# Hybrid decoder trunk: in the third and eleventh up panel, both chunk pairs with seven products stand one chunk later

## The chip, the cores and the metric

The kernel runs on one core of one Trainium2 chip. The metric is the device time of one execution in microseconds (us); for the kernel before it is the median of 3 runs. All arithmetic is fp32.

## What is computed

Two layers over 256 tokens of width 2048, each with attention beside a cross-attention over 256 memory tokens, and then a channel mixer. Only the channel mixer bears on the change:

```python
def conv_ffn(h, w_up, conv_w, conv_b, w_down):
    u = causal_dwconv(h @ w_up, conv_w, conv_b)      # width 3 over the tokens
    a, val = split_cols(u, [FFN_HIDDEN, FFN_HIDDEN])  # 5632 each
    return (jax.nn.silu(a) * val) @ w_down

def reference(...):
    for i in range(DEPTH):                            # DEPTH = 2
        ...                                           # attention adds to x
        h = rmsnorm(x, norm_ffn[i])
        x = x + conv_ffn(h, ffn_w_up[i], ffn_conv_w[i], ffn_conv_b[i], ffn_w_down[i])
    return rmsnorm(x, norm_final)
```

## The kernel before

**Three matmuls for one product.** Both factors are kept as a rounded part ("hi") and the rest ("lo"). A product takes hi times hi, lo times hi and hi times lo, three matmuls. The activations are kept so already (buffers A and B, 16 chunks of 128 rows). The weights are split as they arrive: SyncE's queue (SP) loads a chunk into a slot of the ring `raws` (L246, or L455 for a pair), ScalarE makes hi (L256, or L404), VectorE makes lo (L257, or L405). The rings have slots of 128 x 1024 words: in the mixer eight for raw weights (five and three guests) and six each for hi and lo.

**Up panels.** The up-projection of a layer is done in eleven panels, `up_pair(j)` for j = 0, 4, ..., 40. Each computes 512 columns of `a` and 512 of `val` (two halves `h_`) for 256 tokens (two blocks `b`), and takes the 16 chunks of the contraction one after the other. The third panel is j = 8, the eleventh and last j = 40. Panels 0 to 16 come first, then two down panels (`down_pair`), then panels 20 to 28 and so on; after panel 40 come the last down panels.

**Pairs with seven products.** An ordinary chunk k takes four products (2 blocks by 2 halves) of three matmuls, 12 in all. Two chunks k and k+1 that stand in `sums` are taken together by Winograd's form of Strassen's scheme: seven products p1 to p7 of three matmuls, 21 instead of 24. Its weight sums are built on VectorE in place in the pair's two raw slots `ra` and `rb` (L461 to L464), and there are four splits (`split_more`, L404 and L405): `w1` and `w2` of the weights as they are, `w3` and `w4` of the sums. `w3` feeds p5 and p7, `w4` feeds p6 and p4. The sums of the activations (`usum`) were made ahead. Panels with j // 4 in `MORE_IN` (1, 2, 5 to 10) take two pairs, (6,7) and (11,12), the others one, (6,7).

**Where the pairs stand.** `pair_steps` lays down the order of the chunks. Its argument `ahead` says how far ahead of its own place a pair is taken:

```python
        while at < n:
            if at + ahead in sums:
                plan.append(at + ahead)
                at += 2
            else:
                plan.append(single.pop(0))
                at += 1
```

`up_pair` passes `2 * second`: 2 in a panel with two pairs, otherwise 0.

**Banks and ends of a panel.** Eight PSUM banks are used: the products p1, p5, p7, p6 ("fast") in four of them and p2, p3, p4, x ("slow", into which the ordinary chunks also go) in the other four. `flip` exchanges the two sets from panel to panel, so that the fast products of the third and the eleventh panel lie in `ps_o`, `ps_s`, `ps_s`, `ps_t`, where the slow ones of the next panel go. After the last pair `early` adds up the fast banks (L1527 to L1534); after the last chunk `late` adds each slow bank (L1538), and VectorE turns the blocks (L1489). GpSimd's queue writes the turned blocks to DRAM (L674) and reads them back in another order (L679).

**Conv work.** What a panel has produced is convolved and gated in the next panel and beyond: 12 tap products on ScalarE for each half (L1442), two adds on VectorE (L1449), the silu (L1455) and the gating (L1462 and the split L552 and L553). `tick(share)` hands out these steps after each yield of `pair_steps`: after an ordinary chunk a share of 1.7 (panels with two pairs) or 1.45, after a pair two ticks with a share of 0. A half costs 10.2 shares. Its steps come due 7 or 8 ticks after the panel's end, the read-back 3 ticks after it, if the slot has been read by then.

**Order on the engines.** Each engine takes its instructions in a fixed order, which a planner lays down at build time from simulated times and priorities (`high_priority` lifts the weight loads and splits; `issue_after` puts one instruction behind another). So matmuls of neighbouring chunks can stand between the products of a pair, and a later chunk's cast ahead of a pair's split.

Of the kernel before, what the change touches and what calls it, by code (L numbers as in the profile page):

```python
# [40 lines left out]
RAW_GUESTS = 3  # L41
PUT_OFF = {16: 21}
FIRST_DOWN = (10,)


LEVELS = (64, 16, 4)
# [105 lines left out]
def _trunk(ctx: ExitStack, tc: tile.TileContext, xt, xtok, memt, wp, wgu, gns, gfin, cnv, par, msk, out):  # L152
# [1217 lines left out]
    def down_pair(l, p, f, src, sums, flip, pool, temps, then=None):  # L1370

        def early(bank):
            t0, t1 = temps()
            S.activation(t0, bank["p1"], AF.Copy)
            add_to(f)(0, t0)
            V.tensor_tensor(t0, bank["p6"], t0, ALU.add)
            V.tensor_tensor(t1, bank["p7"], t0, ALU.add)
            add_to(f)(1, t1)
            add_to(f + 1)(1, t1)
            add_to(f + 1)(1, bank["p5"])  # L1380
            V.tensor_tensor(t0, bank["p5"], t0, ALU.add)
            add_to(f + 1)(0, t0)

        def late(b, h, a):
            held_back = then is not None and h and not b and then.rooms is not None
            with tc.issue_after(then.turned[-1].ins) if held_back else nullcontext():
                add_to(f + h)(b, a)
            if then is not None:
                then(f + h, b)

        return pair_steps(where["down", l, p, f], src, sums, flip, pool, early, late)
# [26 lines left out]
    def ffn(l, nx, h, m, more, ys, zs, landing, then, pool, temps, last=None, spare=None):  # L1418
        with tc.tile_pool(name=f"ffn{l}", bufs=1) as fp:
# [14 lines left out]
            count = [0, 0, 0]  # L1434
# [43 lines left out]
            def scale(b):  # L1478
                return nx.col()[:, b : b + 1]

            def turn(j, wait):

                count[0] += 1
                slot = count[0] % 2
                y, z = ys[slot], zs[slot]

                def evac(b, a):
                    with tc.high_priority(offset=AHEAD):
                        turned_last[0] = V.transpose(y[:, :, :, b, :], a.rearrange("p (k c i) -> p c k i", c=4, i=32))  # L1489
                    if b:  # L1490
                        away = far_away(dram, flat(y), T, nc.gpsimd)
                        back = lambda: away(flat(z))
                        steps = [(0.5, lambda s=s, c=c, i=i: tap_of(j, s, c, i, slot)) for n in ((1, 2), (0,))
                                 for s in range(2) for c in range(2) for i in n]
                        steps += [(1.0, lambda: add_tap(1)), (1.0, lambda: add_tap(2)), (0.5, silu),
                                  (1.0, lambda: gated(j, 0)), (0.7, lambda: gated(j, 1))]
                        returns.append((clock[0] + 3, slot, back, [(clock[0] + wait, *step) for step in steps]))

                return evac
# [18 lines left out]
            def up_pair(j):  # L1518

                count[2] += 1  # L1520
                second = j // 4 in MORE_IN
                turns = [turn(j + 2 * h_, PUT_OFF.get(j) or (7 if not h_ and j // 4 + 1 in MORE_IN else 8)) for h_ in range(2)]
                u = {}

                def early(bank):
                    u.update({(b, h_): temps(2 * b + h_) for b in range(2) for h_ in range(2)})
                    S.activation(u[0, 1], bank["p1"], AF.Copy)  # L1527
                    S.activation(u[0, 0], bank["p1"], AF.Copy, scale=scale(0))
                    V.tensor_tensor(u[0, 1], bank["p6"], u[0, 1], ALU.add)
                    V.tensor_tensor(u[1, 0], bank["p7"], u[0, 1], ALU.add)  # L1530
                    V.tensor_tensor(u[0, 1], bank["p5"], u[0, 1], ALU.add)
                    V.tensor_tensor(u[1, 1], bank["p5"], u[1, 0], ALU.add)
                    for b, h_ in ((0, 1), (1, 0), (1, 1)):
                        S.activation(u[b, h_], u[b, h_], AF.Copy, scale=scale(b))  # L1534

                def late(b, h_, a):
                    with tc.issue_after(turned_last[0].ins) if h_ and not b else nullcontext():
                        V.scalar_tensor_tensor(u[b, h_], a, scale(b), u[b, h_], ALU.mult, ALU.add)  # L1538
                    turns[h_](b, u[b, h_])

                return pair_steps(where["up", l, j], h, {k: up_sums[k] for k in (*SEVEN_UP, SEVEN_MORE)[: 1 + second]},
                                  count[2] % 2, pool, early, late, 2 * second)

            def first(k):
                {2: lambda: nx.land(landing[0]), 3: nx.take, 8: nx.col,
# [5 lines left out]
            def drive(steps, share=1.45):  # L1551
                for k in steps:
                    tick(share if k >= 0 else 0.0)

            def drive_up(j):
                drive(up_pair(j), 1.7 if j // 4 in MORE_IN else 1.45)
# [3 lines left out]
            for k in up_pair(0):  # L1560
                first(k)
            done = 4
            for p, (lo, hi) in enumerate(PARTS[:-1]):
# [4 lines left out]
                for f in (0, 2):  # L1568
                    count[2] += 1
                    drive(down_pair(l, p, f, src, {c - lo: t for c, t in sums.items() if (c in FIRST_DOWN) == (f == 0)}, count[2] % 2, pool,  # L1570
                                    lambda: (temps(0), temps(1))))
# [93 lines left out]
    with tc.tile_pool(name="stash", bufs=1) as st:  # L1665
# [4 lines left out]
        with tc.tile_pool(name="turn1", bufs=1) as tp:  # L1670
# [4 lines left out]
            def temps(i):  # L1675
                return fixed[i] if i < 2 else tp.tile([P, 512], F32, name="temp", tag=f"temp{i}")
# [149 lines left out]
```

## Time and profile before

| | us |
|---|---|
| runs | 2212.15, 2214.28, 2210.77; median 2212.15 |
| profiled execution | 2209.92 |
| its span | 2208.0 |
| TensorE busy in the span | 2194.4 |
| VectorE busy | 1832.8 |
| ScalarE busy | 1436.7 |
| GpSimd busy | 136.9 |

In the profile's rows PE is TensorE's matmuls, PEld its weight loads, DVE is VectorE, ACT ScalarE, POOL GpSimd and SP SyncE; L12 is line 12 of the kernel. `acc`, `ps_o`, `ps_s` and `ps_t` are PSUM banks; `whi` and `wlo` are the split weights (`more`, `moremk` and `moremv` are the sixth slots of those rings); `usum` are the sums of activations. A row of a timeline merges like instructions that follow each other. Matmul ends are modelled, so the distance of the starts tells more than the busy time.

### The profile page before, as it was taken

How to read it: one execution, taken by the hardware profiler on the slowest of the kernel's cores; microseconds unless marked ns; L12 is line 12 of the kernel's file. 1: busy time of each engine (PE TensorE's matmuls, PEld its weight loads, DVE VectorE, ACT ScalarE, POOL GpSimd, SP SyncE). 2: the span in 40 equal slices, each digit the busy share in tenths (PEclk: the TensorE clock that was granted, in tenths of full speed). 3: DMA queues.
4: the chain of work that ended last, by engine and by line, in shares of the span. 5: the costliest groups of instructions: out<-in, count | busy, mean ns of one | idle time of the engine just before them, and what ended most of it. 6: DMA issues, size and time to landing. Idle time of an engine off the chain costs nothing.

```text
span 2208.0 us, 30096 instructions
## 1 busy us (share of the span) xinstructions
PE 2194.4 (99%) x10285; PEld 1845.4 (84%) x10285; DVE 1832.8 (83%) x2731; ACT 1436.7 (65%) x2282; POOL 136.9 (6%) x257
## 2 busy tenths in 40 slices
PE   9999999999999999999999999999999999999998
PEld 7888888888888888888888998888878888888886
DVE  7768976679998889889887669668999888988996
ACT  6655655557785668647765555455878567765774
POOL 0000000001100010001010000000100000101000
PEclk9999999999999999999999999999999999999999
DMA  9866666777776667767777667776787667766682
GB/s 367 253 224 220 194 212 225 253 233 245 264 253 231 199 220 257 237 202 236 250 241 244 222 199 240 232 244 224 257 264 240 219 199 246 241 230 209 232 284 96
DMA packets 166289, 515.40 MB, mean 233 GB/s; under 512 B 20780, under 2 KB 42552, under 8 KB 166136
## 3 DMA queue, kind: packets, MB, share of 16 engines
q1 hardware_dynamic: 149064, 460.99, 63.3%
q0 software_dynamic: 16496, 51.71, 7.5%
q8 instruction: 80, 1.31, 0.2%
q10 hardware_dynamic: 576, 0.79, 0.1%
q14 instruction: 73, 0.60, 0.1%
HBM read 469.62 MB, written 43.79 MB: 233 GB/s over the span
## 4 chain that ended last, share of the span: by engine, by line
PE 97%; DMA 1%; DVE 1%; ACT 1%; issue 0%; SPq 0%; DVEq 0%; ACTq 0%
PE acc L434 28%; PE acc L361 26%; PE ps_s L434 15%; PE ps_o L434 7%; PE ps_t L434 7%; PE acc L332 3%; PE acc L287 3%; PE ps_s L361 2%; PE acc L391 2%; PE acc L285 1%; DMA raw<-wp 1%; PE ps_s L1059 0%; DMA far<-blk 0%; DVE wlo L405 0%; PE ps_o L725 0%
## 5 line engine op out<-in xcount | busy, mean ns | idle before, releaser
L257 DVE TENSOR_TENSOR wlo<-raw,whi 128x1024 fp32r<-128x1024 f32 (+2 forms) x613 | 729.9, 1198 | 221.9 <-ACT whi L256 208.8
L256 ACT ACTIVATE whi<-raw 128x1024 fp32r<-128x1024 f32 (+2 forms) x613 | 636.3, 1044 | 371.3 <-PE acc L361 146.0
L361 PE MATMUL acc<-whi,B 128*128 128x512 f32 (+3 forms) x1248 | 290.8, 369 | 0.0
L361 PEld LDWEIGHTS acc<-whi,B 128*128 128x128 f32 x1248 | 226.8, 188 | 28.1
L404 ACT ACTIVATE whi<-raw 128x1024 fp32r<-128x1024 f32 (+1 forms) x154 | 146.9, 957 | 121.0 <-PE ps_t L434 42.1
L405 DVE TENSOR_TENSOR wlo<-raw,whi 128x1024 fp32r<-128x1024 f32 (+1 forms) x154 | 167.7, 1091 | 20.8 <-ACT whi L404 12.4
L434 PE MATMUL acc<-whi,mix 128*128 128x512 f32 x668 | 171.9, 390 | 0.4 <-ACT whi L256 0.2
L434 PE MATMUL acc<-whi,B 128*128 128x512 f32 x650 | 170.2, 389 | 0.0
L361 PE MATMUL acc<-wlo,B 128*128 128x512 f32 (+3 forms) x624 | 159.1, 369 | 0.0
L434 PEld LDWEIGHTS acc<-whi,mix 128*128 128x128 f32 x668 | 125.2, 188 | 27.4 <-ACT whi L256 0.9
L434 PEld LDWEIGHTS acc<-whi,B 128*128 128x128 f32 x650 | 121.9, 188 | 25.6 <-ACT whi L256 0.3
L1442 ACT ACTIVATE tap<-fvt,cw 128x256 f32<-128x256 f32 x264 | 123.8, 531 | 9.4 <-DMA fvt<-far 8.7
L1442 ACT ACTIVATE tap<-yzu,cw 128x256 f32<-128x256 f32 x264 | 123.6, 529 | 4.6 <-DMA yzu<-far 4.0
L361 PEld LDWEIGHTS acc<-wlo,B 128*128 128x128 f32 x624 | 114.2, 188 | 14.6
L1449 DVE TENSOR_TENSOR tap<-tap,tap 128x1024 f32<-128x1024 f32 x88 | 106.9, 1215 | 0.0
L434 PE MATMUL acc<-wlo,B 128*128 128x512 f32 x325 | 95.9, 389 | 0.0
L434 PE MATMUL acc<-wlo,mix 128*128 128x512 f32 x334 | 95.5, 389 | 0.0
L434 PE MATMUL ps_s<-whi,mix 128*128 128x512 f32 x332 | 92.3, 389 | 0.0
L434 PE MATMUL ps_s<-whi,B 128*128 128x512 f32 x282 | 79.2, 389 | 0.0
L434 PEld LDWEIGHTS acc<-wlo,mix 128*128 128x128 f32 x334 | 62.7, 188 | 13.4 <-DVE wlo L405 0.4
L434 PEld LDWEIGHTS ps_s<-whi,mix 128*128 128x128 f32 x332 | 62.3, 188 | 12.9
L434 PEld LDWEIGHTS acc<-wlo,B 128*128 128x128 f32 x325 | 61.0, 188 | 12.7
(545 smaller groups left out, 4282.4 us busy)
## 6 DMA issues: line engine op xcount, KB each, us to landing
raw<-wp SPq DMA_DIRECT2D x741, 512.0 KB, 4.5
fvt<-far POOLq DMA_DIRECT2D x100, 128.0 KB, 5.1
raw<-wp SPq DMA_DIRECT2D x32, 384.0 KB, 3.6
far<-yu POOLq DMA_DIRECT2D x22, 512.0 KB, 3.5
far<-yzu POOLq DMA_DIRECT2D x22, 512.0 KB, 3.7
yzu<-far POOLq DMA_DIRECT2D x88, 128.0 KB, 4.5
raw<-wp SPq DMA_DIRECT2D x24, 388.0 KB, 3.5
x<-xtok SPq DMA_DIRECT2D x8, 512.0 KB, 6.9
```

Of the source, the lines that this page charges most:

```text
L256: casts.append(S.activation(hi[:, s], raw[:, s], AF.Copy))
L257: lows.append(V.tensor_tensor(lo[:, s], raw[:, s], hi[:, s].bitcast(F32), ALU.subtract))
L285: mm = TE.matmul(acc[p][c][:, :T], w[:, s], both[:, 0, :], start=False, stop=end and j == 3)
L287: mm = TE.matmul(acc[p][c], w[:, s], both, start=u == j == 0, stop=end and j == 3)
L332: mm = TE.matmul(acc[b][:, :n], src[kcs[j] - base][:, part, b * P : (b + 1) * P], w, start=u == 0 and low == part == j == 0, stop=u == end ...
L361: mm = TE.matmul(acc[b][:, :n], src[kc - base][:, part, b * P : (b + 1) * P], ready[low][:, j * room : j * room + n], start=i == low == pa ...
L391: mm = TE.matmul(acc[b][:, :n], src[kc - base][:, part, b * P : (b + 1) * P], w, start=i == low == part == j == 0, stop=i == end and low = ...
L404: casts.append(S.activation(hi[:, :n], src, AF.Copy))
L405: lows.append(V.tensor_tensor(lo[:, :n], src, hi[:, :n].bitcast(F32), ALU.subtract))
L434: r = TE.matmul(bank[name], x, w, start=name not in begun, stop=last)
L1442: S.activation(by_run(taps[i][:, s, c, i:]), zs[slot][:, :, 2 * c + s], AF.Copy if i else AF.Identity, bias=0.0 if i else w[3], scale=w[2 ...
L1449: V.tensor_tensor(taps[0], taps[0], taps[n][:, :, :, :T], ALU.add)
```

## The change

A table `UP_AHEAD` gives `ahead` for two of the panels, 1 instead of 2. Their order of chunks goes from 0 1 2 3 (6,7) 4 5 8 (11,12) 9 10 13 14 15 to 0 1 2 3 4 (6,7) 5 8 9 (11,12) 10 13 14 15, in both layers. The ticks follow the chunks: the two ticks without a share that go with a pair come one tick later as well.

```diff
@@ -41,6 +41,7 @@
 RAW_GUESTS = 3
 PUT_OFF = {16: 21}
 FIRST_DOWN = (10,)
+UP_AHEAD = {8: 1, 40: 1}
 
 
 LEVELS = (64, 16, 4)
@@ -1539,7 +1540,7 @@
                     turns[h_](b, u[b, h_])
 
                 return pair_steps(where["up", l, j], h, {k: up_sums[k] for k in (*SEVEN_UP, SEVEN_MORE)[: 1 + second]},
-                                  count[2] % 2, pool, early, late, 2 * second)
+                                  count[2] % 2, pool, early, late, UP_AHEAD.get(j, 2 * second))
```

## The prediction

> **What bounds the kernel now.** I read the page first, then busy time by stretch, then Tensor's timeline where a stretch had holes, then the chain of waits and the other engines' timelines at those places.
>
> ```profile
> span 2208.0 us, 30096 instructions
> ## 1 busy us (share of the span) xinstructions
> PE 2194.4 (99%) x10285; PEld 1845.4 (84%) x10285; DVE 1832.8 (83%) x2731; ACT 1436.7 (65%) x2282; POOL 136.9 (6%) x257
> ```
>
> Tensor is busy in 99% of the span, and the change removes no matmul, so only Tensor's pauses can be won. The profiled execution took 2209.92 us (1.92 beside its span); the median of the runs is 2212.15, 2.23 above it. A difference worked out on the trace is taken off the median unchanged.
>
> The next rows are stretches by start:end, then length, then busy us of PE, PEld, DVE, ACT, POOL. The first four are the two changed panels (third panel, layer 0 and 1; eleventh panel, layer 0 and 1); the fifth is layer 0's second panel.
>
> ```profile
> 541.60:583.70 42.10, 42.10 (x187) 34.90 (x186) 38.54 (x46) 32.08 (x50) 5.50 (x10) 1.00 0.66 222
> 1578.40:1622.10 43.70, 42.72 (x187) 34.54 (x187) 38.87 (x46) 32.04 (x50) 5.47 (x10) 1.00 0.72 222
> 1030.70:1075.00 44.30, 43.41 (x190) 35.29 (x190) 41.77 (x54) 34.20 (x54) 5.48 (x10) 1.00 0.73 236
> 2069.00:2113.60 44.60, 43.50 (x191) 35.33 (x191) 41.81 (x54) 34.27 (x54) 5.49 (x10) 1.00 0.69 228
> 497.00:540.00 43.00, 43.00 (x191) 35.62 (x190) 41.89 (x55) 34.32 (x55) 5.48 (x10) 1.00 0.83 278
> ```
>
> The third panel of layer 0 has no hole; the other three have. Tensor's timeline (start, duration, tile; in brackets the idle time before it) puts all three at the same work: the products p6 and p4 of the panel's second pair.
>
> ```profile
> 1604.96 0.61 PE L434 MATMUL ps_s<-wlo,usum 128*128 128x512 f32 x2
> 1606.30 0.72 PE L434 MATMUL ps_t<-whi,usum 128*128 128x512 f32 x2 [0.73 <-ACT whi L404]
> ...
> 1607.75 0.50 PE L434 MATMUL ps_t<-wlo,usum 128*128 128x512 f32 x1 [0.26 <-DVE wlo L405]
> 1608.09 0.40 PE L434 MATMUL acc<-wlo,A 128*128 128x512 f32 x1
> ```
>
> ```profile
> 1057.26 0.61 PE L434 MATMUL ps_s<-wlo,usum 128*128 128x512 f32 x2
> 1058.33 0.73 PE L434 MATMUL ps_t<-moremk,usum 128*128 128x512 f32 x2 [0.46 <-ACT moremk L404]
> ...
> 1059.96 0.51 PE L434 MATMUL ps_t<-moremv,usum 128*128 128x512 f32 x1 [0.43 <-DVE moremv L405]
> ```
>
> ```profile
> 2095.56 0.61 PE L434 MATMUL ps_s<-wlo,usum 128*128 128x512 f32 x2
> 2096.83 0.73 PE L434 MATMUL ps_t<-more,usum 128*128 128x512 f32 x2 [0.66 <-ACT more L404]
> ...
> 2098.47 0.50 PE L434 MATMUL ps_t<-more,usum 128*128 128x512 f32 x1 [0.44 <-DVE more L405]
> ```
>
> The bracketed idle times add to 2.98 us. Measured from start to start it is more, as Tensor restarts slowly. The rate comes from a dense stretch of the chain (start, us, what):
>
> ```profile
> 1578.37 10.89 PE acc L434 x48
> ...
> 1595.99 8.23 DMA raw<-wp
> ```
>
> 48 matmuls in 10.89 us are 0.227 each, a chunk of 12 is 2.72. In each fence the lo product of ps_t would follow the first row's two matmuls, its own two hi ones and two of p4: six matmuls, 1.36 us after the first row. It came 2.79 us after it, 1.43 late, and by the same count 1.34 and 1.55 late in the other two; the matmul behind it then comes after 0.34 (1607.75 to 1608.09) where 0.23 is usual. Lost are 1.54, 1.45 and 1.66, together 4.65. That is all that these panels have to give, and 0.2% of the median, about what a measurement of this kernel can tell from no change, is 4.42.
>
> **Why p6 is late.** p6 needs the fourth split of its pair (L404 on Scalar, L405 on Vector). Both engines take their instructions in a fixed order:
>
> ```profile
> 1604.24 1.06 ACT L256 ACTIVATE whi<-raw 128x1024 fp32r<-128x1024 f32 x1 [4.75 <-DMA raw<-wp]
> 1605.21 1.04 ACT L404 ACTIVATE whi<-raw 128x1024 fp32r<-128x1024 f32 x1
> 1605.34 1.23 DVE L257 TENSOR_TENSOR wlo<-raw,whi 128x1024 fp32r<-128x1024 f32 x1 [3.19 <-ACT whi L256]
> 1606.48 1.22 DVE L405 TENSOR_TENSOR wlo<-raw,whi 128x1024 fp32r<-128x1024 f32 x1
> ```
>
> Ahead of that split (1605.21) stands the cast of a later single chunk (1604.24), and it waits 4.75 us for its weights. Their load, the chain's DMA row, was issued at 1595.99. By the ring of eight raw slots, the third single after the second pair reuses the first pair's second slot, which is free when Vector has split it for the last time: the first pair's tail on Vector sets off the load that later blocks p6. In layer 0 the same order stands, the load came at 565.80, and p6 found its split ready:
>
> ```profile
> 565.80 1.06 ACT L256 ACTIVATE whi<-raw 128x1024 fp32r<-128x1024 f32 x1 [2.94 <-DMA raw<-wp]
> 568.79 0.62 PE L434 MATMUL ps_t<-whi,usum 128*128 128x512 f32 x2
> ```
>
> So the loss is a lag of one to two us at the second pair.
>
> **The change, part by part.** Four panels run changed (two places in the list, two layers). The chunk order goes from 0 1 2 3 (6,7) 4 5 8 (11,12) 9 10 13 14 15 to 0 1 2 3 4 (6,7) 5 8 9 (11,12) 10 13 14 15. Nothing is added or removed.
>
> *One more chunk ahead of both pairs.* Tensor reaches p6 12 matmuls later, 2.72 us. Until then Vector has one chunk split more: from 1605.34 to 1606.48, 1.14 us with the overlap, 1.23 at most; Scalar one cast, 1.06. Three singles with conv work stand between the pairs as before, as that work comes due in the sixth or seventh step and the pair's own steps give it no share. The lead grows by 2.72-1.23 = 1.49 us on Vector, 1.66 on Scalar. Against the lateness of 1.43, 1.34 and 1.55 a lead of 1.49 covers two and leaves 0.06. Where Vector or Scalar are held by Tensor's releases instead, the lead is smaller; where all hangs on Tensor, nothing is won.
>
> *The queues that the pair is moved past.* SP's queue has the same 16 loads in a panel, chunk 4's ahead of the pair's two now. The raw slots shift with the chunks: after the second pair the first single again has a slot freed early, the second and third the slots of the first pair. So the blocking order itself stays. The load that blocked took 8.23 us against this median:
>
> ```profile
> raw<-wp SPq DMA_DIRECT2D x741, 512.0 KB, 4.5
> ...
> yzu<-far POOLq DMA_DIRECT2D x88, 128.0 KB, 4.5
> ```
>
> I keep 8.23, since POOL's read-back may still lie over it; at 4.5 the lead would grow by 3.7 more. In the panel behind the third, one step of conv work more is left over (1.7 of 20.4 shares) and the second read-back is called one step, 2.72 us, later. Its first reader comes due four steps (10.9 us) on, and a read-back lands in 4.5: nothing. If that cover went, it would be up to 2.72 us in two places.
>
> *Four chunks instead of five behind the second pair.* The early sums (L1527 to L1534) have 2.72 us less until the next panel's p4 overwrites the bank that L1532 reads. Third panel, layer 0 and layer 1, then the eleventh:
>
> ```profile
> 580.76 0.68 DVE L1532 TENSOR_TENSOR temp<-ps_s,temp 128x512 f32<-128x512 f32 x1
> 584.21 0.62 PE L434 MATMUL ps_s<-whi,B 128*128 128x512 f32 x2
> ```
>
> ```profile
> 1619.18 0.68 DVE L1532 TENSOR_TENSOR temp<-ps_s,temp 128x512 f32<-128x512 f32 x1
> 1622.51 0.61 PE L434 MATMUL ps_s<-whi,mix 128*128 128x512 f32 x2
> ```
>
> ```profile
> 1070.07 0.68 DVE L1532 TENSOR_TENSOR temp<-ps_s,temp 128x512 f32<-128x512 f32 x1
> 1075.07 1.07 PE L434 MATMUL ps_s<-moremk,A 128*128 128x512 f32 x4
> ```
>
> Spare are 584.21-581.44 = 2.77, 1622.51-1619.86 = 2.65 and 1075.07-1070.75 = 4.32. If the sums keep their distance to p6, 2.72 less leaves 0.05, -0.07 and 1.60: a cost of 0.07. If one Vector split of 1.23 slips ahead of L1532, the two third panels pay 1.18 and 1.30.
>
> **The sum.** 4.65 to win, less 0.06 uncovered, less 0.07 at the panel's end. The instruction order comes from a planner that weighs everything anew, so I do not expect three clean places: I leave each one wait of the smallest size in the rows, 0.26, together 0.78. That is 4.65-0.06-0.07-0.78 = 3.74: 2209.92 would become 2206.2 and the median 2208.4. Ends: all of it, 2207.5; nothing won and both third panels paying, 2212.15+2.48 = 2214.6.
>
> **A rule against it.** Vector is busy for 41.77 of 44.30 us in the eleventh panel, 94%. The Trainium skill, "Perfetto Trace Analysis", section "Identifying the Most-Contended Engine", takes occupancy as a fair measure of how near Vector is to its limit, judges Tensor by its weight loads (here 35.29 us, 80%), and names the engine with the highest figure as the bottleneck; by that the panel would be Vector's, an exchange of order would win nothing, and the time would stay 2212.2. The trace speaks against it: in the fifth stretch Vector is busy for 41.89 of 43.00 us, 97%, and Tensor for all 43.00.
>
> **The rivals.**
> - *Vector is simply full* (7%). What p6 no longer waits for, a later matmul does; 2212.2. For it: 94% there. Against it: the 97% stretch without a pause.
> - *The lag moves along* (20%). Scalar's casts wait for Tensor to free the split buffers; if the first pair's splits hang on that, and not on Vector's backlog, all comes 2.72 us later with Tensor, the blocked load too, and p6 waits as now; also if the planner sets a later cast ahead of p6's again, so that the change does not do what it says. 2212.2, within 1 us. For it: the slot mapping shifts with the chunks. Against it: the early sums, transposes and conv adds of the panel before, on Vector, do not move.
> - *The bank at the panel's end* (11%, slower). L1532 slips behind two splits (2.46 us) in all four panels: the third ones pay 2.41 and 2.53, the eleventh 0.86 each, 6.66 in all, against 4.65-0.06 won at best: 2214.2; with p6's waits unimproved as well, 2218.8. It decides from the point where the sums come more than 1.2 us later behind p6 than now. For it: the spare of 0.05 us. Against it: fewer splits are left to be put between.
>
> **How the numbers follow.** Forecast 62%, its own range 2206.4 to 2210.5; of it 26 points lie below 2207.7 (0.2% faster), since a shorter blocked load or a fuller cover takes the whole 4.65, and the runs themselves differ by 3.5 us. The first two rivals are all within 0.2%; of the last, whose two times lie on either side of 2216.6, 6 points are slower by more than that and 5 within. So faster 0.26, same 0.68, slower 0.06. The range reaches from 1.5 us under the full gain, 2206.0, to the paid panel ends, 2214.6.
>
> **What would show it.** Right: no idle in front of the ps_t products of the second pair in those panels, their stretches near 42.2 us for 186 matmuls, the cast ahead of the fourth split no longer waiting for a load. Wrong: the same bracketed waits 2.72 us further on; or idle at the first ps_s matmul of the next panel with L1532 as the releaser; or a wait in panels that were not touched, which the planner's new order would have made.

## The result and the profile after

| us | kernel before | changed kernel |
|---|---|---|
| runs beside each other, median (lowest to highest) | 2210.64 (2208.77 to 2214.28) | 2205.43 (2204.14 to 2206.67) |
| ratio of the times, 95% interval | 1 | 0.9977 [0.9968, 0.9986] |
| profiled execution | 2209.92 | 2206.67 |
| its span | 2208.0 | 2204.9 |

The changed kernel is faster by 0.23%, 5.2 us by the medians and 3.1 by the two spans. Forecast were 2208.4, and 2206.0 to 2214.6 as the range: the sign is right, the time is lower than forecast and lies below the range.

The page of the changed kernel, its first lines:

```profile
span 2204.9 us, 30083 instructions
...
PE 2192.4 (99%) x10285; PEld 1845.2 (84%) x10285; DVE 1836.0 (83%) x2731; ACT 1437.9 (65%) x2282; POOL 137.3 (6%) x257
```

The matmuls are the same 10285; the span and Tensor's busy time are both a few us less. Behind the table's new line every line number is one higher than before: the cast and lo of an ordinary chunk are L257 and L258 now, those of a pair L405 and L406, the matmuls L435, the tap products L1443, the early sums L1528 to L1535.

Busy time by stretch in the changed kernel, for the same four panels in the prediction's order (start:end, length, then busy us of PE, PEld, DVE, ACT, POOL):

```profile
541.60:583.70 42.10, 42.10 (x187) 34.85 (x187) 39.81 (x47) 31.53 (x51) 5.50 (x10) 1.00 0.71 236
1576.90:1619.10 42.20, 42.20 (x188) 34.94 (x187) 40.27 (x48) 32.68 (x53) 5.49 (x10) 1.00 0.72 246
1029.00:1073.00 44.00, 44.00 (x196) 36.44 (x195) 43.06 (x57) 34.79 (x56) 5.50 (x10) 1.00 0.73 242
2065.90:2109.90 44.00, 44.00 (x196) 36.44 (x195) 42.62 (x55) 33.65 (x55) 5.52 (x10) 1.00 0.71 241
```

Tensor is busy for the whole of all four; before it missed 0.98, 0.89 and 1.10 us in three of them by the same column. Tensor's list of waits in the changed kernel, from the first up panel to the end of layer 1's mixer, is short (engine, line, what ended the wait: us in total, times, longest):

```profile
PE acc L435 <- ACT whi L257: 1.5, 1, 1.5
PE acc L362 <- DVE wlo L258: 0.2, 1, 0.2
PE acc L392 <- DVE wlo L258: 0.2, 1, 0.2
```

Nothing waits at `ps_t` any more. The first row is layer 1's first up panel, which had a pause before too; the other two are new and stand in the down panels behind the last up panel.

Counted from start to start as in the prediction (what a step takes beyond 0.227 us a matmul), the mixer's pauses are, in us:

| profiled execution | third, layer 0 / 1 | eleventh, layer 0 / 1 | layer 1's first panel | closing down panels, layer 0 / 1 | span |
|---|---|---|---|---|---|
| before | 0 / 1.63 | 1.45 / 1.65 | 1.21 | 0 / 0 | 2208.0 |
| changed | 0 / 0 | 0 / 0 | 1.78 | 0.62 / 0.51 | 2204.9 |

So 4.73 us went from the four panels (the prediction's 4.65, and 0.08 that stood beside them), and 0.19 from layer 0's first panel; 1.13 came in the closing panels and 0.57 in layer 1's first panel. That is 3.2 us less, where the spans differ by 3.1.

Where the fourth split stands now. Scalar's timeline of the changed kernel, third panel of layer 1, answers to the rows at 1604.24 of before:

```profile
1603.01 1.07 ACT L257 ACTIVATE more<-raw 128x1024 fp32r<-128x1024 f32 x1 [1.83 <-PE acc L435]
1603.98 0.59 ACT L1443 ACTIVATE tap<-yzu,cw 128x256 f32<-128x256 f32 x1
1604.47 1.05 ACT L405 ACTIVATE whi<-raw 128x1024 fp32r<-128x1024 f32 x1
1605.42 2.00 ACT L257 ACTIVATE whi<-raw 128x1024 fp32r<-128x1024 f32 x2
```

and Tensor's:

```profile
1607.34 1.52 PE L435 MATMUL acc<-more,mix 128*128 128x512 f32 x6
1608.70 0.61 PE L435 MATMUL ps_s<-wlo,usum 128*128 128x512 f32 x2
1609.16 0.62 PE L435 MATMUL ps_t<-whi,usum 128*128 128x512 f32 x2
...
1612.10 0.39 PE L435 MATMUL ps_t<-wlo,usum 128*128 128x512 f32 x1
...
1621.40 0.62 PE L435 MATMUL ps_s<-whi,mix 128*128 128x512 f32 x2
```

The last cast ahead of the fourth split (1603.01) waits for Tensor to free a buffer, not for a load. It fills the buffer `more`, and from 1607.34 on Tensor takes 12 matmuls with it, the first of the four ordinary chunks behind the pair; the load that came late before was, by the ring of raw slots, the third's. The split ends at 1605.52 and p6 starts at 1609.16: 3.6 us of slack, where before it was late. In layer 0's eleventh panel the fourth split ends at 1058.95 and p6 starts at 1063.44, 4.5 us of slack.

### The profile page after: what moved, and what is told of

It is laid out like the page before. It is cut to its first block, busy times and chain, and to the rows that moved or that the text cites. A ratio compares the mean times of both kernels' runs of the same rounds, so it can differ in the third digit from the quotient of the medians.

```text
span 2204.9 us, 30083 instructions
## 1 busy us (share of the span) xinstructions
PE 2192.4 (99%) x10285; PEld 1845.2 (84%) x10285; DVE 1836.0 (83%) x2731; ACT 1437.9 (65%) x2282; POOL 137.3 (6%) x257
## 3 DMA queue, kind: packets, MB, share of 16 engines
q8 instruction: 80, 1.31, 0.2%
## 4 chain that ended last, share of the span: by engine, by line
PE 98%; DMA 1%; DVE 0%; ACT 0%; SPq 0%; issue 0%; DVEq 0%; ACTq 0%
PE acc L435 30%; PE acc L362 26%; PE ps_s L435 15%; PE ps_o L435 8%; PE ps_t L435 7%; PE acc L288 3%; PE acc L333 3%; PE ps_s L362 2%; PE acc L392 2%; PE acc L286 1%; DMA raw<-wp 1%; PE ps_s L1060 0%; PE ps_o L726 0%; DMA far<-blk 0%; PE ps_s L726 0%; PE ps_s L1333 0%
## 5 line engine op out<-in xcount | busy, mean ns | idle before, releaser
L258 DVE TENSOR_TENSOR wlo<-raw,whi 128x1024 fp32r<-128x1024 f32 (+2 forms) x613 | 732.1, 1202 | 221.3 <-ACT whi L257 205.5
L257 ACT ACTIVATE whi<-raw 128x1024 fp32r<-128x1024 f32 (+2 forms) x613 | 636.6, 1044 | 368.0 <-PE acc L362 138.2
L405 ACT ACTIVATE whi<-raw 128x1024 fp32r<-128x1024 f32 (+1 forms) x154 | 146.6, 952 | 121.4 <-PE ps_t L435 32.5
L406 DVE TENSOR_TENSOR wlo<-raw,whi 128x1024 fp32r<-128x1024 f32 (+1 forms) x154 | 167.4, 1089 | 17.9 <-ACT whi L405 12.8
L435 PE MATMUL acc<-whi,mix 128*128 128x512 f32 x666 | 171.2, 389 | 1.5 <-ACT whi L257 1.5
L435 PE MATMUL acc<-whi,B 128*128 128x512 f32 x650 | 170.9, 389 | 0.0
L435 PEld LDWEIGHTS acc<-whi,mix 128*128 128x128 f32 x666 | 124.9, 188 | 27.8 <-ACT whi L257 1.9
L435 PEld LDWEIGHTS acc<-whi,B 128*128 128x128 f32 x650 | 122.0, 188 | 25.4
L1443 ACT ACTIVATE tap<-fvt,cw 128x256 f32<-128x256 f32 x264 | 123.9, 532 | 8.2 <-DMA fvt<-far 7.1
L1443 ACT ACTIVATE tap<-yzu,cw 128x256 f32<-128x256 f32 x264 | 123.8, 531 | 7.5 <-DMA yzu<-far 6.2
L435 PE MATMUL acc<-wlo,B 128*128 128x512 f32 x325 | 96.2, 389 | 0.0
L435 PE MATMUL acc<-wlo,mix 128*128 128x512 f32 x333 | 95.0, 389 | 0.0
L435 PE MATMUL ps_s<-whi,mix 128*128 128x512 f32 x332 | 92.6, 389 | 0.0
L435 PE MATMUL ps_s<-whi,B 128*128 128x512 f32 x282 | 79.3, 389 | 0.0
L435 PEld LDWEIGHTS acc<-wlo,mix 128*128 128x128 f32 x333 | 62.5, 188 | 13.0
L435 PEld LDWEIGHTS ps_s<-whi,mix 128*128 128x128 f32 x332 | 62.3, 188 | 12.9
L435 PEld LDWEIGHTS acc<-wlo,B 128*128 128x128 f32 x325 | 61.0, 188 | 12.7
```

The lines of the kernel that those rows point to most:

```text
L257: casts.append(S.activation(hi[:, s], raw[:, s], AF.Copy))
L258: lows.append(V.tensor_tensor(lo[:, s], raw[:, s], hi[:, s].bitcast(F32), ALU.subtract))
L405: casts.append(S.activation(hi[:, :n], src, AF.Copy))
L406: lows.append(V.tensor_tensor(lo[:, :n], src, hi[:, :n].bitcast(F32), ALU.subtract))
L435: r = TE.matmul(bank[name], x, w, start=name not in begun, stop=last)
L1443: S.activation(by_run(taps[i][:, s, c, i:]), zs[slot][:, :, 2 * c + s], AF.Copy if i else AF.Identity, bias=0.0 if i else w[3], scale=w[2 ...
```

## The experiments

Two theories were set against each other. *Lead*: the pairs come one chunk later on Tensor, and the 1.5 us so gained on Vector and Scalar cover the late split. *Order*: the planner's new order no longer puts a cast whose load comes late ahead of the fourth split; the pair's place matters only as it brings that about.

**The change once more** (`e1_again`, the changed kernel itself).

> The changed kernel once more, timed beside the kernel before on one chip. The two traces differ by 3.1 us of span (2208.0 to 2204.9), the medians of the runs by 5.2. If the trace tells all, the difference is 3 to 3.6 us here. If something that these two executions did not show is also won, it is 4.5 to 6 us. In the trace: no idle before the ps_t products of the second pair in the four panels, and one pause of about 0.5 us each behind the last up panel (near 1115 and 2151 us).

Measured: 2205.99 (2204.90 to 2206.92) against 2210.42 (2208.02 to 2215.75) for before, ratio 0.9979 [0.9971, 0.9988]; span 2204.8, pauses 1.43 in layer 1's first panel and 0.62 and 0.48 in the closing panels, none in the four panels. The gain holds; 4.4 us by the medians lie between the two ranges that were expected. The changed kernel's times spread over 2.0 us (11 executions), those of before over 7.7 (33).

**The third panel alone** (`e2_third`).

```diff
-UP_AHEAD = {8: 1, 40: 1}
+UP_AHEAD = {8: 1}
```

> Only the third panel is changed. Each panel for itself: Tensor's pause of 1.54 us in layer 1's third panel goes, the two in the eleventh panels (1.45 and 1.66) stay, and no new pause comes behind the last up panel: 1.5 us faster. If the gain is made elsewhere, in the planner's new order, the stretches of the third panel alone do not tell it: more than 3 us, or nothing.

Measured: 2206.87, ratio 0.9983 [0.9975, 0.9992], 3.6 us faster, more than the third panel has to give. Tensor's waits in its trace:

```profile
PE ps_t L435 <- ACT more L405: 0.9, 1, 0.9
PE ps_t L435 <- ACT moremk L405: 0.6, 1, 0.6
PE ps_t L435 <- DVE moremv L406: 0.4, 1, 0.4
PE ps_t L435 <- DVE more L406: 0.4, 1, 0.4
```

The third panel's wait is gone, the eleventh's are as before (1.63 and 1.86 from start to start). There is no wait in the closing panels, nor, in this execution, in layer 1's first panel (1.21 before). That last 1.2 to 1.5 us makes up for what the third panel cannot give; whether it is the new order or chance, one execution does not tell. The spans differ by 2.5 us (2208.0 to 2205.5).

**The eleventh panel alone** (`e3_eleventh`).

```diff
-UP_AHEAD = {8: 1, 40: 1}
+UP_AHEAD = {40: 1}
```

> Only the eleventh panel is changed. Each panel for itself: the pauses of 1.45 and 1.66 us in the eleventh panels go, 1.54 stays in layer 1's third panel, and the two new pauses of about 0.5 us behind the last up panel are there: 3.1 - 1.0 = 2.1 us faster. If the new pauses belong to the third panel's change, they are missing here: 3.1 us.

Measured: 2206.99, ratio 0.9987 [0.9978, 0.9995], 3.4 us faster by the medians where 2.1 were expected. The eleventh panel has no pause, and the closing ones are there (0.61 and 0.51): they belong to the eleventh's change. The unchanged third panel was to show the old wait in layer 1; it shows 0.11. Scalar's timeline of this kernel there:

```profile
1602.13 1.07 ACT L257 ACTIVATE whi<-raw 128x1024 fp32r<-128x1024 f32 x1 [3.23 <-DMA raw<-wp]
1603.10 1.05 ACT L405 ACTIVATE whi<-raw 128x1024 fp32r<-128x1024 f32 x1
```

The order is that of before, the cast still waits for its load ahead of the fourth split, but 3.23 us instead of 4.75; the split was ready at 1604.15, and p6 started at 1604.84. The wait's size thus goes with the load's, and one execution is a poor measure of it. The two halves of the change, 3.6 and 3.4 us by the medians, are together more than both at once (5.2 and 4.4); their intervals, 1.8 to 5.5 and 1.1 to 4.9 us, are too wide to add them up.

**Three more profiled executions of the kernel before** (`before_b`, `before_c`, `before_d`, no edit), for that reason.

> The kernel before, one more execution with its trace. In five panels whose order was the same the pause at the second pair and the time of the load that the cast waits for moved together: 5.73 and 1.45 us, 5.92 and 1.64, 5.94 and 1.66, 6.14 and 1.87. If that load sets the pause, each execution has other pauses and each tenth of a us more of the load is a tenth more of pause. If order alone sets it, the pauses are those of the first trace, 1.54, 1.45 and 1.66, within 0.1.

> The kernel before, another execution with its trace; the same two expectations as for before_b. The span should follow the sum of the pauses in the three panels and at the start of layer 1's first panel (4.65 and 1.2 us in the first trace, span 2208.0).

> The kernel before, a third one; the same expectations. If the medians of the runs, 5.2 and 4.4 us apart, tell more than the traces' 3.1 because the pauses are longer in most executions than in the first trace, at least two of these three have a larger sum of pauses than 4.65 + 1.2.

Measured, pauses as above:

| | time | span | third, layer 0 / 1 | eleventh, layer 0 / 1 | the four together |
|---|---|---|---|---|---|
| before | 2209.92 | 2208.0 | 0 / 1.63 | 1.45 / 1.65 | 4.73 |
| before_b | 2209.85 | 2208.0 | 0 / 0.68 | 1.82 / 1.95 | 4.45 |
| before_c | 2207.47 | 2205.6 | 0 / 0 | 1.31 / 0.82 | 2.13 |
| before_d | 2211.85 | 2210.0 | 1.04 / 1.09 | 1.70 / 2.88 | 6.71 |

The sum goes from 2.1 to 6.7 us, and the span goes with it. With layer 1's first panel (1.21, 1.47, 1.44 and 1.49) the four executions have 5.94, 5.92, 3.57 and 8.20 us of pauses. So of the three new ones one has more than the first, one the same and one less, not two more as the last expectation asked: that longer pauses are the rule is not shown. The chain of waits names the load in three of the four, not in before_c; for before, eleventh panel of layer 0 and of layer 1 (start, us, what):

```profile
1049.56 5.73 DMA raw<-wp
...
2087.86 5.94 DMA raw<-wp
```

for before_b:

```profile
1049.50 6.12 DMA raw<-wp
...
2087.50 6.24 DMA raw<-wp
```

for before_d:

```profile
1050.29 5.99 DMA raw<-wp
...
2088.62 7.16 DMA raw<-wp
```

In layer 0 the load of 5.73, 5.99, 6.12 us stands beside a pause of 1.45, 1.70, 1.82; in layer 1 5.94, 6.24, 7.16 beside 1.65, 1.95, 2.88. Each tenth of a us in the load is a tenth in the pause.

In the eleventh panel the load is only a part of it. Scalar's timeline there in before (layer 0) and in before_c (layer 1):

```profile
1055.32 2.01 ACT L256 ACTIVATE whi<-raw 128x1024 fp32r<-128x1024 f32 x2 [0.53 <-DMA raw<-wp]
1057.24 1.04 ACT L404 ACTIVATE moremk<-raw 128x1024 fp32r<-128x1024 f32 x1
```

```profile
2091.40 2.00 ACT L256 ACTIVATE whi<-raw 128x1024 fp32r<-128x1024 f32 x2
2093.30 1.04 ACT L404 ACTIVATE more<-raw 128x1024 fp32r<-128x1024 f32 x1
```

Two casts stand ahead of the fourth split here, 2.0 us of work. The first waits 0.53 us for its load in before; in before_c it doesn't wait at all, and 0.82 us of pause are there all the same. So in the eleventh panel most of the pause is the order itself, and a late load adds to it. In layer 1's third panel one cast stands ahead, and there a wait of 3.06 us for the load (before_c) costs Tensor nothing, 3.81, 4.22 and 4.75 cost 0.68, 1.09 and 1.63.

**The order alone** (`e4_order`): the pairs stay where they were in before, and the casts of the ordinary chunks behind the second pair are put behind the fourth split's on Scalar.

```diff
+HOLD = (8, 40)
...
+                fourth = casts[-1].ins
...
-                w = split_unit(units[k])
+                behind = hold and not any(e in plan[plan.index(k):] for e in end)
+                with tc.issue_after(fourth) if behind else nullcontext():
+                    w = split_unit(units[k])
...
-                                  count[2] % 2, pool, early, late, 2 * second)
+                                  count[2] % 2, pool, early, late, 2 * second, j in HOLD)
```

> The kernel before with its pairs where they were; only the casts of the single chunks behind the second pair are queued on Scalar behind the pair's fourth split in the third and eleventh panels (an order on the same engine, no wait). Theory 'the cast that waits for its load stands ahead': the pauses before the ps_t products go here too (4.6 us of them), though no pair is moved: 3 to 5 us faster, as the change. Rival 'lead' (what the prediction counted: Scalar and Vector come 1.5 us too late as a whole, and only one more chunk ahead gives them time): the fourth split is not done earlier, at least 3 us of the pauses stay, and the time is within 1.5 us of the kernel before.

Measured: 2207.26, ratio 0.9984 [0.9975, 0.9993], 3.2 us faster. No product of a second pair waits in any of the four panels, though no pair was moved. Scalar's timeline in layer 0's eleventh panel, and Tensor's below it:

```profile
1054.26 1.05 ACT L405 ACTIVATE moremk<-raw 128x1024 fp32r<-128x1024 f32 x1
1055.42 2.01 ACT L257 ACTIVATE whi<-raw 128x1024 fp32r<-128x1024 f32 x2
...
1058.38 1.05 ACT L257 ACTIVATE whi<-raw 128x1024 fp32r<-128x1024 f32 x1
```

```profile
1057.27 0.62 PE L435 MATMUL ps_t<-moremk,usum 128*128 128x512 f32 x2
...
1058.18 0.39 PE L435 MATMUL ps_t<-moremv,usum 128*128 128x512 f32 x1
...
1059.49 2.11 PE L435 MATMUL acc<-whi,B 128*128 128x512 f32 x8 [0.70 <-ACT whi L257]
```

The fourth split goes straight through, and p6 and its lo products follow without a gap. The late load is still there, in this kernel's chain of waits:

```profile
1049.12 6.28 DMA raw<-wp
```

Behind its cast, one more cast and two early sums now stands the next ordinary chunk's cast (1058.38), for which Tensor waits: 0.97 in layer 0 and 1.27 in layer 1 are left of the eleventh's 1.45 and 1.65. Order decides who waits; in the eleventh panel this exchange alone leaves a pause, in the third it leaves none in either layer.

The edit asks for one exchange, but the planner lays out everything behind it anew. The traces of before and of this kernel first part in their order of instructions at 565 us, in layer 0's third panel. In each of the four panels, up to p6, they differ in one thing: the fourth split's cast stands further ahead on Scalar, and its lo half with it on Vector; the orders of Tensor and of the loads are the same there. So the pause in front of p6 is the order's, while the 3.2 us are those of the whole new layout.

**A strict order** (`e5_strict`): as above, but every ordinary chunk behind the second pair queues behind the one ahead of it.

```diff
-                with tc.issue_after(fourth) if behind else nullcontext():
+                with tc.issue_after(casts[-1].ins) if behind else nullcontext():
```

> The kernel before with its pairs where they were; on Scalar every single chunk behind the second pair is cast in the order of the chunks, behind the fourth split, in the third and eleventh panels. Holding the casts behind the fourth split alone left pauses of 0.98 and 1.27 us in the eleventh panels, now before the first single chunk, whose cast stood behind a cast that waited for its load. Theory 'order': with the first single's cast ahead of it these go too, no pause is left in the four panels or behind the last up panel, and the time is 1 to 2 us below the changed kernel's two pauses there: 4.4 to 6 us faster than before. Rival 'the load itself is late': the pause is found again at the second or third single, and the time is that of the kernel with the fourth split alone, 3.2 us faster.

Measured: 2207.43, ratio 0.9983 [0.9975, 0.9992]. No pause is left in the four panels, with the pairs in their old places; 0.77 and 1.51 stand in the closing down panels instead. So the four panels can be cleared with the pairs in their old places, and what is won there comes back in part behind them, as with the change itself. The time, 3.3 us faster by the medians, is not the 4.4 to 6 that were expected of it.

**Both pairs two chunks later** (`e6_two_later`), the far end of the same step.

```diff
-UP_AHEAD = {8: 1, 40: 1}
+UP_AHEAD = {8: 0, 40: 0}
```

> The pairs two chunks later than before in the third and eleventh panels (6th and 11th place, three chunks behind the second). The prediction's price for the panel's end: the early sums keep their distance to p6 and lose 2.72 us more. In the changed kernel's trace the second ps_s matmul of the next panel comes 2.85 us after the last early sum in layer 1's third panel, so 0.1 to 0.2 us are left, and one Vector split in between costs 1.1 us: pauses at the first ps_s matmuls of the next panel of 0 to 1.2 us in each of the third panels. If the planner again puts the early sums nearer to p6 and the ps_s products later, there is no pause at the panel's end, and the time is that of the changed kernel within 1 us.

Measured: 2212.02, ratio 1.0004 [0.9995, 1.0013]: neither expectation, the gain is gone and the pauses are elsewhere. No pause in the four panels nor at the next panel's `ps_s`, where the bank was to be missed; but the closing panels pause for 3.07 and 3.06 us and an up panel of layer 1 (at 1649 us) for 1.0. Tensor's longest wait in layer 0's closing panel:

```profile
1115.95 2.14 PE L362 MATMUL acc<-whi,mix 128*128 128x512 f32 x8 [1.87 <-ACT whi L257]
```

**All panels with two pairs one chunk later** (`e7_all`).

```diff
-                                  count[2] % 2, pool, early, late, UP_AHEAD.get(j, 2 * second))
+                                  count[2] % 2, pool, early, late, second)
```

> All panels with two pairs take them one chunk later, not the third and eleventh alone. The other panels have no pause to win. If a place one chunk later is better by itself (more time for the splits), nothing changes there and the time is the changed kernel's within 0.7 us. If what counts is which cast the planner puts ahead of which split, new pauses of 0.5 to 2 us come up in some of the twelve other panels, and it is 1 to 5 us slower than the changed kernel.

Measured: 2211.4, ratio 1.0001 [0.9992, 1.001]. In the third and the eleventh panel, whose pairs stand as in the changed kernel, pauses are back: 1.08, 1.52, 0.87 and 2.11. The twelve other panels, where new ones were expected, have none. What Scalar does in the third panel of layer 1,

```profile
1599.76 1.32 ACT L1443 ACTIVATE tap<-yzu,cw 128x256 f32<-128x256 f32 x3 [4.52 <-DMA yzu<-far]
1600.97 1.04 ACT L405 ACTIVATE whi<-raw 128x1024 fp32r<-128x1024 f32 x1
1601.92 3.57 ACT L1443 ACTIVATE tap<-yzu,cw 128x256 f32<-128x256 f32 x8
1605.40 2.00 ACT L405 ACTIVATE whi<-raw 128x1024 fp32r<-128x1024 f32 x2
```

and what Tensor does there:

```profile
1602.07 0.73 PE L435 MATMUL ps_t<-whi,usum 128*128 128x512 f32 x2
...
1606.49 0.73 PE L435 MATMUL acc<-whi,A 128*128 128x512 f32 x2 [0.36 <-ACT whi L405]
```

Here tap products that waited 4.52 us for a read-back stand ahead of the first pair's last split (1600.97, p6 at 1602.07 comes late), and eight more ahead of the second pair's second and third (1605.40, the wait at 1606.49). The same place of the pairs with another order on Scalar gives waits again: the place alone isn't enough.

**One more queue** (`e8_queue`): the strict order, and the write and read-back ahead of layer 1's mixer on GpSimd's queue instead of SP's, against the pause in its first panel.

```diff
-        n, then = preparing("ffn1", bufA, tp, dram)
+        n, then = preparing("ffn1", bufA, tp, dram, queue=nc.gpsimd)
```

> As the kernel that casts in the order of the chunks, and the turned blocks ahead of layer 1's first panel go over GpSimd's queue, not SyncE's, where the first panel's pair loads stood behind a read-back that waited 5.8 to 6.9 us for its write. The pause near 1508 us (0.8 to 1.8 us in the traces) goes: 1 us faster than with the casts in order alone. If the loads are late for another reason, or GpSimd's descriptors come later, the pause stays or moves to the norm's values and nothing is won.

Measured: 2211.86, ratio 1.0002 [0.9993, 1.0011]. The pause that it was to remove grew to 3.07, and the third panel of layer 1 has one of 1.95, at its first pair's p6, behind tap products that waited 3.76 us for a read-back. The DMA issues between 1490 and 1512 us, in the changed kernel:

```profile
raw<-wp SPq DMA_DIRECT2D x7, 512.0 KB, 4.3
far<-blk SPq DMA_DIRECT2D x1, 512.0 KB, 5.8
```

and in this one:

```profile
raw<-wp SPq DMA_DIRECT2D x7, 512.0 KB, 8.5
yzu<-far POOLq DMA_DIRECT2D x8, 128.0 KB, 7.3
far<-blk POOLq DMA_DIRECT2D x1, 512.0 KB, 4.0
```

Once they no longer stand in one queue, the weight loads take 8.5 us (median of 7) instead of 4.3, and 4.6 in e5_strict, whose order of casts this kernel has. More falls into these 22 us too: eight read-backs instead of four, 5.6 MB instead of 4.2. The Trainium skill, "DMA: Bandwidth & Descriptors", section "Issuing engines are not separate DMA queues", says that transfers started by different engines run on the same 16 DMA engines and interleave; these rows fit that. No version tried is faster than the changed kernel.

## Why the prediction was right in sign and wrong in size

**Right: the place and the cause.** Only the pauses at p6 and p4 of the second pair were to be won, and they are what went (stretches 42.10 and 42.20 us without idle, as foreseen). That the wait was the fixed order on Scalar, a cast that waits for its load ahead of a split that is ready, is shown by e4_order: in these panels, up to p6, it changes that order, with the lo halves' on Vector that follow it, and nothing else, and p6 no longer waits. The prediction read the third panel's rows and took them for the eleventh's as well, where two casts stand ahead and the wait for the load is 0.53 us of it. The Trainium skill, "PSUM — Partial Sum Buffer", section "Engine vs sequencer instructions", has the queues of Scalar and Vector strictly first in, first out; the traces agree: in layer 1's third panel one cast that waited for its load, 4.75 us in before and 3.23 in e3_eleventh, held up the ready split behind it.

**Wrong: "so the blocking order itself stays", and with it the 0.06 of uncovered lead and the 0.78 of leftover waits.** The prediction took the ring of raw slots to put the late load ahead of the fourth split again, and reckoned with a lead of 1.49 us. In the changed kernel the cast ahead of that split is the first chunk's behind the pair, not the third's, and its load is there (the fence at 1603.01); the slack at p6 is 3.6 and 4.5 us, not 0. The three leftovers were a guess for the planner's part, put at the size of the smallest row; the planner did move things, but not to there. In the changed kernel's two traces the four panels have no leftover, so nothing shows the 0.78 there. e7_all shows that this could have gone otherwise: with the same places, its order brings the waits back.

**Wrong, at little cost: the panel's end, −0.07.** The early sums did not keep their distance to p6. Vector's timeline of the changed kernel, third panel of layer 1:

```profile
1613.20 0.68 DVE L1530 TENSOR_TENSOR temp<-ps_t,temp 128x512 f32<-128x512 f32 x1
...
1617.26 0.69 DVE L1532 TENSOR_TENSOR temp<-ps_s,temp 128x512 f32<-128x512 f32 x1
1617.86 0.69 DVE L1533 TENSOR_TENSOR temp<-ps_s,temp 128x512 f32<-128x512 f32 x1
```

From the lo product of `ps_t` to the end of the last sum from `ps_s` (L1533 here, L1532 before) it was 1619.86 − 1607.75 = 12.1 us before and is 1618.55 − 1612.10 = 6.45 now; the spare up to the next `ps_s` matmul (1621.40) is 2.85 us, not −0.07. Vector runs without a gap there in both traces (from 1608.29 before, from 1604.11 now), so what set the sums' time is their place in its order, not p6.

**Missed: the closing panels, +1.13.** The last row of the prediction named "a wait in panels that were not touched", but no term had it. The chain of waits of the changed kernel behind layer 0's eleventh panel:

```profile
1112.84 1.12 DVE wlo L258
1113.95 0.60 DVE x L523
1114.56 1.15 DVE wlo L258
...
1115.75 3.06 PE acc L362 x12
```

A lo split with an add to `x` (L523) between it and the split before comes 0.4 us late for the first closing down panel; the same stands at 2151.01 in layer 1. It belongs to the eleventh panel's change (in e3_eleventh, not in e2_third), and two chunks later it is 3.07 (e6_two_later). That it grows because work of the panel's end is pushed into the closing panels is the likely reading; it wasn't tried by itself.

**Wrong in size: 4.65 as "all that these panels have to give".** It is one execution's value of a wait that goes from 2.1 to 6.7 us in four of them, 4.5 in the mean. By the traces the account is 4.5 won less 1.1 in the closing panels, 3.4; the mean spans differ by 3.1 (2207.9 for before in four, 2204.85 for the change in two). That this is near the sum's 3.74 is luck: 0.91 was taken off for costs that came to nothing, and 1.1 came where no term stood. The medians say 5.2 and, in e1_again, 4.4, with intervals of 3.1 to 7.1 and 2.7 to 6.4 us (the ratios' ends times 2210). The traces' value lies inside both.

**Wrong: "a difference worked out on the trace is taken off the median unchanged", and with it the range.** The two profiled executions are 3.25 us apart, the medians 5.21. The one of before, 2209.92, was 0.72 below its median (2210.64); the changed kernel's, 2206.67, was the slowest of its eight, 1.24 above its median (2205.43). These two distances are the whole 1.96 between the two differences; which pauses the executions without a trace had isn't known, so the cause stays open. The range's low end, 2206.0, was 1.5 under the full gain off a median of three, 2212.15. Beside the changed kernel the same program's median was 2210.64: the starting point alone moved by 1.5 us. From there the prediction's sum, 3.74, gives 2206.9 and the full gain 2206.0, still 0.6 above what was measured.

**The rivals.** *Vector is simply full* is refuted: in layer 0's eleventh panel Vector is busy for 43.06 of 44.00 us, 98%, and Tensor for all of it; the rule of the Trainium skill, "Perfetto Trace Analysis", section "Identifying the Most-Contended Engine", that the prediction weighed would have the panel bound by Vector. *The lag moves along* is refuted for the change by the 3.6 us of slack, though it is what e7_all did. *The bank at the panel's end* did not pay here, nor two chunks later.

## What to carry to other kernels

When a dense engine waits for a step that is ready but for its engine's queue, look at the instructions ahead of it: their work and any wait of theirs for a load are passed on to it, and an exchange of order can take that away (here wholly in the third panel; in the eleventh a stricter order was needed). Where a planner lays the order out anew, predict which instruction stands ahead, not only how much lead is won, and look for the cost behind the panel where the pushed work ends. A pause that ends on a DMA should be priced from several executions, and the base of a forecast of 0.2% too.

## What the chip showed that was not expected

The same 512 KB weight load, in the same place of the same program, took 5.7 to 6.1 us in layer 0's eleventh panel, 5.9 to 7.2 in layer 1's, and 7.3 to 8.2 in layer 1's third, in the three executions of before whose chain shows it, and once the cast in the way is late for Tensor, each further tenth is handed on in full. The changed kernel's times spread less (2.0 us in 11 executions, before 7.7 in 33), but e5_strict, whose four panels have no pause either, spread over 4.9, so that the pauses make up the spread is not shown. And Vector at 98% over 44 us cost Tensor nothing.
